# Projection chunks of 512 columns, kept split weights, and transposed x scaled on GpSimd in a one-core mixer step

## The chip, the cores and the metric

The kernel runs on one core of a Trainium2 chip. The metric is device time in microseconds for one execution; smaller is better. Five engines work side by side: PE (TensorE, matrix products), DVE (VectorE), ACT (ScalarE), POOL (GpSimd) and SP (SyncE, which here only issues transfers). Each engine runs its own list of instructions strictly in order, and waits for the others through semaphores.

## The reference, cut to what matters

```python
xn = rmsnorm(x, g_pre)                  # x: 2048 prompt tokens and 8x4 sample tokens, 1024 wide
proj = xn @ w_in                        # 1024 -> 38*128 columns
a_c, b_c, g_c, x_r, g_r, q, g_q = split(proj)       # 6, 6, 6, 6, 6, 4, 4 tiles of 128 columns
u = a_c * sigmoid(b_c)                  # then 31-tap depthwise conv, layernorm, silu, times silu(g_c)
...                                     # x_r: 4-tap conv, gates, linear recurrence, times silu(g_r)
...                                     # q: attention to 256 memory tokens, times silu(g_q)
out = concat([c, rr, o]) @ w_out        # 2048 -> 1024
y = x + rmsnorm(out, g_post)
```

All of it is float32, and besides y the new caches (the last conv rows, the recurrence state, memory keys and values) are outputs.

## The kernel before, in words

A float32 product is made of three products in a rounded type: each operand is split into a high part and a low rest, and `mm3` (L103) issues hi·hi, hi·lo and lo·hi into the same bank. `split` (L108) makes the parts: ACT copies the high part, DVE subtracts it from the source for the low part.

Phase 1 makes the projections and the three branches, in two parts of 1024 tokens; the first part also carries the 32 sample tokens. In each part the normalised x stands transposed (columns of x on the partitions) and split in `xh` and `xl`, in chunks of CW = 352 tokens (352, 352, 320; the last of the first part has 32 sample tokens more). `proj(m)` (L388) makes one 128-column tile of the projection: `load_w` (L236) loads 512 KB of raw weights on SP's queue, ACT and DVE split them into wh and wl, and for each chunk PE issues 8 k-steps of three matmuls into one PSUM bank; then an evacuation function runs. The tiles are named by their group: M_A, M_B (conv), M_GC, M_XR, M_GR, M_Q, M_GQ. There are 38 of them, so the weights are loaded and split 38 times in each part.

The x of the first part: the token rows of a chunk are loaded (`chunk_rows`), ACT sums their squares (`row_rs`, L213), DVE and POOL make the reciprocal root (L214, L215), DVE scales the rows (L221), PE transposes them eight times (L230), ACT and DVE take the split parts out of PSUM (L232, L233). The x of the second part: the row sums are made ahead (`part_stats`), x is loaded already transposed (`scaled_cols`, L346), DVE scales it with a broadcast row (L350), ACT and DVE split it (`split_cols`, L356, L357).

The order of the steps within a part is a string (ORDER): G is a conv tile pair with its GLU (`glu`), X, S, O belong to the recurrence, C is a conv gate (`conv_gate`), q and o are attention, M and V the memory keys and values, N the memory's normalisation, R the row sums of part 2; "G2:3" advances a step by three yields. G0 is the first step, and in it the tiles M_B and M_A run together, chunk by chunk. A scheduler that simulates the engines then sets each engine's own order; `high_priority` moves weight loads ahead. Pools of buffers (bufs=) decide when a tile's space comes free.

Branch results go to DRAM scratch (mixd, convd) through POOL's queue. Phase 2 (from 1035 us) keeps the split w_out resident and runs 17 blocks of tokens: output projection on 512 columns, norm, residual.

Of the kernel before, what the change touches and what calls it, by code (L numbers as in the profile page):

```python
# [32 lines left out]
EPS = 1e-6  # L33
CW = 352
CONV_LOW = 3000
MIX_HIGH = 500
# [3 lines left out]
NLC = 7  # L40
NCK = 5
NKC = 2
# [5 lines left out]
    "G0 N M1 X0:3 M0 X0:3 M2 X0:3 L X0 G1 G2:3 V G2 S0:2 S0:1 M3 S0:1 S0 C0 O0 C1 q0:3 G3:1 q0 G3 o0 R X1:7 X1 S1:1 G4 S1:1 S1:1 C2 C4 S1 O1 q1:3 G5:1 q1 G5:2 o1 G5 q3:3 C3:1 q3 C3 q2:3 o3:1 q2 o3 o2 C5",  # L48
    "G0:1 G0 s0 s1 p v0 X0 v1 G1 S0:1 G2:1 S0:1 G2 S0:1 S0 C0 O0 q0:3 G3:1 q0 G3:1 o0 G3 G4:3 X1 S1:1 G4 S1:1 S1 C1 O1 q1:3 G5:1 q1 G5 o1 q3:3 q2:1 q3 q2:2 o3:1 q2 o3 o2 C5 C4 C2 C3",
)  # L50
# [18 lines left out]
def hybrid_mixer_kernel(ctx, tc, x, xT, mem, consts, lnc, ccT, lcT, ckT, cv, w_in,  # L69
# [47 lines left out]
    def phase1():  # L117
# [117 lines left out]

        def load_w(src, ahead=None):  # L236
            with tc.high_priority(offset=W_HIGH if ahead is None else ahead):
                raw = pw.tile([P, KD, P], F32, tag="wr", name="wr", bufs=WR)
                sp.dma_start(raw, src)
                wh = pw.tile([P, KD, P], F32R, tag="wh", name="wh")  # L240
                wl = pw.tile([P, KD, P], F32R, tag="wl", name="wl")
                split(wh, wl, raw)
            return wh, wl
# [73 lines left out]
        def chunk_rows(part, c):  # L317
            alloc = flat_lc if c == len(part_chunks[part]) - 1 else big
            return load_rows([[x[t:t + w, :] for _, w, t in b] for b in row_blocks(part, c)], alloc)

# [15 lines left out]

        def scaled_cols(part, c):
# [3 lines left out]
            xs = [lc() for _ in range(3)]  # L341
            for a, w, tok in pieces(part, c, 0, n + ns):
                pool.dma_start(rb[:, a:a + w], rsd[0, tok:tok + w].partition_broadcast(P))
# [16 lines left out]
        for part in range(2):  # L360
            t0 = part * PART
            has_s = part == 0
            chunks = part_chunks[part]

            xh, xl = [], []
# [5 lines left out]
            ready[FIRST] = load_w(w_in[FIRST], 0)  # L371
            for c, (c0, n, ns) in enumerate(chunks):
                h = px.tile([P, KD, CW], F32R, tag="xh", name="xh")
                l = px.tile([P, KD, CW], F32R, tag="xl", name="xl")
                w = n + ns
                hi, lo = (lambda k: h[:, k, :w]), (lambda k: l[:, k, :w])
                if has_s:
                    if c + 1 < len(chunks):
                        rows[c + 1] = chunk_rows(0, c + 1)
                    if c == 0:  # L380
                        ready[M_A] = load_w(w_in[M_A], 0)
# [4 lines left out]
                xh.append(h)  # L386
                xl.append(l)
            def proj(m, evac):  # L388
                wh, wl = ready.pop(m) if m in ready else load_w(w_in[m])
                for c, (c0, n, ns) in enumerate(chunks):  # L390
                    w = n + ns
# [16 lines left out]
            def glu(i):  # L408
# [18 lines left out]
                def ev_a(c, ps):  # L427
                    ah = ck()
                    act.activation(ah[:, :ps.shape[1]], ps, AF.Copy, scale=0.5)
                    for dst, src in parts(c, ah):  # L430
                        dve.scalar_tensor_tensor(dst, dst, 1.0, src, op0=ALU.add, op1=ALU.mult)
# [53 lines left out]
            def lru_in(g):  # L485
                xrb = []
                lsb = LH + PART
                for i in range(3):
                    ch = 3 * g + i
                    xb = xslot()  # L490
                    sview = xb[:, lsb:].rearrange("p (b s) -> p b s", b=NB)
                    if has_s:
                        dve.memset(xb[:, :LH], 0.0)
                        sp.dma_start(sview[:, :, :LH], lcT[:, ch, :, :])
                    else:
                        act.activation(xb[:, :LH], xhist[:, ch, :], AF.Copy)

                    def ev(c, ps, xb=xb, sview=sview):
                        c0, n, ns = chunks[c]
                        act.activation(xb[:, LH + c0:LH + c0 + n], ps[:, :n], AF.Copy)  # L500
                        if ns:
                            act.activation(sview[:, :, LH:],
                                           ps[:, n:].rearrange("p (b s) -> p b s", b=NB), AF.Copy)

                    yield from proj(M_XR + ch, ev)
                    if has_s:
                        act.activation(xhist[:, ch, :], xb[:, PART:PART + LH], AF.Copy)
                        st_.dma_start(slconvT[:, ch, :, :], sview[:, :, NS:])
# [13 lines left out]
            def lru_scan(g):  # L522
# [13 lines left out]
                def prep(c):  # L536
                    c0, n, ns = chunks[c]
                    w = n + ns
# [30 lines left out]
                yield  # L569
                for c, (c0, n, ns) in enumerate(chunks):  # L570
                    w = n + ns
# [28 lines left out]
                    for i in range(3):  # L600
# [6 lines left out]
                        if ns:  # L607
# [5 lines left out]
                            dve.tensor_copy(xrb[i][1][:, :, :NS], hv)  # L613
                    if c + 1 < len(chunks):
                        nxt = prep(c + 1)
# [78 lines left out]
            def attn_o(h):  # L694
                kv, probs = att.pop(h)
                sg = {}

                def ev_g(c, ps):
                    c0, n, ns = chunks[c]
                    t = ck()  # L700
                    silu2(t[:, :n + ns], ps)
                    if ns:
                        act.activation(sgq[:, h, :], t[:, n:n + ns], AF.Copy)
                    sg[c] = t

                yield from proj(M_GQ + h, ev_g)
                ot = xslot()
                for q4 in range(2):
# [13 lines left out]
                    act.activation(ot[:, q4 * 512:(q4 + 1) * 512], po, AF.Copy)  # L722
                for c, (c0, n, ns) in enumerate(chunks):
                    dve.scalar_tensor_tensor(ot[:, c0:c0 + n], ot[:, c0:c0 + n], 0.5, sg[c][:, :n],
                                             op0=ALU.mult, op1=ALU.mult)
                st_.dma_start(mixd[:, 2 * NT + h, t0:t0 + PART], ot[:, :PART])
# [63 lines left out]
            def conv_gate(i):  # L790
                def ev(c, ps):
                    c0, n, ns = chunks[c]
                    t = pk.tile([P, CW], F32, tag="kc", name="kc", bufs=NKC)[:, :n + ns]
                    act.activation(t, ps, AF.Copy)
# [265 lines left out]
```

## Time and profile before

| | |
|---|---|
| times of three runs | 1429.36, 1429.61, 1431.13 us, median 1429.61 |
| the profiled execution's own time | 1426.34 us |
| its span in the trace | 1424.6 us |
| PE busy | 1405.8 us, 99% of the span |
| DVE, ACT, POOL busy | 1096.5, 681.3, 152.0 us |
| HBM traffic | 106 GB/s over the span |

The span is what the trace covers from first to last instruction; 1.7 us of the profiled execution's time lie around it, and that execution was 3.3 us shorter than the median of the three timed runs. Matmuls are pipelined: a matmul's row shows its whole latency, and the distance between the starts of two neighbours is what one more costs. The times below are microseconds from the span's start.

### The profile page before, as it was taken

To read this page: it belongs to the slowest core of one execution; us is meant where nothing else is said; L and a number is where in the kernel's file an instruction comes from. 1 tells how busy PE (TensorE), PEld (TensorE's weight loads), DVE (VectorE), ACT (ScalarE), POOL (GpSimd) and SP (SyncE) were. 2 spreads that over 40 slices of the span, in tenths; PEclk is the share of its full clock that TensorE was granted. 3 is DMA by queue.
4 is the path that set the end of the run, shared out by engine and by line. 5 is a ranking of instruction groups with operands and counts; after the bars stand their busy time and mean duration, and the time that the engine had idled before them with its cause. 6 is when DMAs were issued, how large, how long until landed. Compare 5 with 4: busy or idle time off the path is not lost.

```text
span 1424.6 us, 21056 instructions
## 1 busy us (share of the span) xinstructions
PE 1405.8 (99%) x8376; PEld 1316.8 (92%) x8376; DVE 1096.5 (77%) x1481; ACT 681.3 (48%) x1326; POOL 152.0 (11%) x233
## 2 busy tenths in 40 slices
PE   9999999999999999999999999999999999999997
PEld 8999999999999999899999999999987788888885
DVE  7797985989889998699989996999874664545532
ACT  7524688346754344238833369434453442332421
POOL 2101121011210101011100110000100000000000
PEclk9999999999999999999999999999999999999998
DMA  6243416132261214621122311421474432423310
GB/s 220 80 83 119 129 64 232 46 93 76 81 191 52 91 65 151 226 88 51 55 89 67 97 49 57 164 88 42 142 250 130 137 118 85 141 93 118 126 60 30
DMA packets 97282, 152.24 MB, mean 107 GB/s; under 512 B 15224, under 2 KB 66800, under 8 KB 97184
## 3 DMA queue, kind: packets, MB, share of 16 engines
q1 hardware_dynamic: 84528, 118.66, 26.5%
q0 software_dynamic: 12656, 32.25, 6.7%
q8 instruction: 65, 1.06, 0.3%
q14 instruction: 33, 0.27, 0.1%
HBM read 114.84 MB, written 36.04 MB: 106 GB/s over the span
## 4 chain that ended last, share of the span: by engine, by line
PE 87%; ACT 5%; DMA 3%; DVE 2%; issue 2%; SPq 0%; POOL 0%; DVEq 0%; POOLq 0%; ACTq 0%
PE bk L104 28%; PE bk L106 28%; PE bk L105 28%; ACT lc L579 1%; PE bk L914 1%; PE bk L714 1%; DMA lc<-in_xT 1%; DVE wl L110 1%; ACT wh L109 1%; DMA big<-in_x 1%; ACT lc L588 0%; ACT lc L584 0%; PE bk L750 0%; DMA lc<-in_x 0%; DMA wr<-in_w_mem 0%
## 5 line engine op out<-in xcount | busy, mean ns | idle before, releaser
L104 PE MATMUL bk<-xh,wh 128*128 128x352 f32 (+1 forms) x1824 | 584.6, 322 | 1.3 <-ACT xh L232 0.7
L105 PE MATMUL bk<-xl,wh 128*128 128x352 f32 (+1 forms) x1824 | 583.6, 320 | 0.0
L106 PE MATMUL bk<-xh,wl 128*128 128x352 f32 (+1 forms) x1824 | 583.0, 321 | 0.4 <-DVE wl L110 0.4
L465 DVE SCALAR_TENSOR_TENSOR big<-ub,cst,big 128x1024 f32<-128x1024 f32 x360 | 457.6, 1283 | 8.9 <-issue 4.4
L104 PEld LDWEIGHTS bk<-xh,wh 128*128 128x128 f32 x1824 | 342.1, 188 | 4.0 <-issue 1.4
L105 PEld LDWEIGHTS bk<-xl,wh 128*128 128x128 f32 x1824 | 343.7, 188 | 1.5 <-issue 0.6
L106 PEld LDWEIGHTS bk<-xh,wl 128*128 128x128 f32 x1824 | 342.6, 188 | 2.1 <-issue 0.8
L105 PE MATMUL bk<-wol,mh 128*128 128x512 f32 x512 | 201.6, 394 | 1.3 <-DVE wol L110 1.3
L104 PE MATMUL bk<-woh,mh 128*128 128x512 f32 x512 | 200.3, 392 | 0.0
L106 PE MATMUL bk<-woh,ml 128*128 128x512 f32 x512 | 199.4, 391 | 0.0
L109 ACT ACTIVATE wh<-wr 128x1024 fp32r<-128x1024 f32 x84 | 89.0, 1059 | 125.6 <-PE bk L105 111.1
L110 DVE TENSOR_TENSOR wl<-wr,wh 128x1024 fp32r<-128x1024 f32 x84 | 103.5, 1232 | 29.1 <-ACT wh L109 24.4
L105 PEld LDWEIGHTS bk<-wol,mh 128*128 128x128 f32 x512 | 96.3, 188 | 20.3 <-DVE wol L110 1.8
L106 PEld LDWEIGHTS bk<-woh,ml 128*128 128x128 f32 x512 | 96.2, 188 | 19.8 <-issue 0.8
L104 PEld LDWEIGHTS bk<-woh,mh 128*128 128x128 f32 x512 | 96.2, 188 | 19.5
L891 ACT ACTIVATE cr<-cr,lnv 128x128 f32<-128x128 f32 (+1 forms) x102 | 40.7, 478 | 150.8 <-DVE cr L889 150.8
L579 ACT ACTIVATE lc<-bk,hb 128x352 f32<-128x352 f32 (+3 forms) x144 | 77.0, 545 | 26.3 <-PE bk L106 23.7
L552 DVE SCALAR_TENSOR_TENSOR lc<-xr,cst,lc 128x352 f32<-128x352 f32 (+2 forms) x126 | 60.4, 522 | 4.6 <-ACT lc L548 4.6
L889 DVE TENSOR_TENSOR cr<-cr,bk 128x768 f32<-128x768 f32 (+1 forms) x17 | 15.6, 918 | 57.1 <-PE bk L888 57.1
L931 DVE TENSOR_TENSOR o<-bk,gpb 128x512 f32<-128x512 f32 (+1 forms) x34 | 23.3, 686 | 32.3 <-ACT sqj L930 32.2
L930 ACT ACTIVATE sqj<-bk 128x512 f32<-128x512 f32 (+1 forms) x34 | 20.1, 592 | 46.0 <-PE bk L106 45.2
L894 DVE TENSOR_TENSOR cr<-cr,mr 128x768 f32<-128x768 f32 (+1 forms) x17 | 15.7, 923 | 32.2 <-ACT cr L891 32.2
(242 smaller groups left out, 1696.2 us busy)
## 6 DMA issues: line engine op xcount, KB each, us to landing
wr<-in_w_in SPq DMA_DIRECT2D x76, 512.0 KB, 3.8
mr<-mixd SPq DMA_DIRECT2D x16, 1024.0 KB, 5.6
raw<-in_w_out SPq DMA_DIRECT2D x16, 512.0 KB, 4.6
xt<-in_x SPq DMA_DIRECT2D x16, 512.0 KB, 5.4
out_y<-xt SPq DMA_DIRECT2D x15, 512.0 KB, 2.7
convd<-big POOLq DMA_DIRECT2D x12, 512.0 KB, 2.9
mixd<-big POOLq DMA_DIRECT2D x12, 512.0 KB, 6.1
cr<-convd SPq DMA_DIRECT2D x16, 384.0 KB, 4.9
```

The source lines that it names most:

```text
L104: pe.matmul(ps, lh, rh, start=first, stop=False)
L105: pe.matmul(ps, lh, rl, start=False, stop=False)
L106: pe.matmul(ps, ll, rh, start=False, stop=last)
L109: act.activation(hi, src, AF.Copy)
L110: dve.tensor_tensor(lo, src, hi.bitcast(F32), op=ALU.subtract)
L465: dve.scalar_tensor_tensor(acc[:, :PART], ub[:, j:j + PART], cw[:, i, j:j + 1], acc[:, :PART], op0=ALU.mult, op1=ALU.add)
L552: dve.scalar_tensor_tensor(o, src(j), lw[:, ch, j:j + 1], o, op0=ALU.mult, op1=ALU.add)
L579: act.activation(dst[lo_:hi_, i, :], ps[lo_:hi_, :], AF.Tanh, scale=0.5, bias=hb[lo_:hi_, a, 3 * g + i:3 * g + i + 1])
L891: act.activation(cr[:, i, :], cr[:, i, :], AF.Silu, scale=lng[:, i:i + 1], bias=lnb[:, i:i + 1])
L894: dve.tensor_tensor(cr, cr, mr[:, :NT, :m], op=ALU.mult)
L930: act.activation(sqj[:m, :], ps[n][:m, :], AF.Square, scale=float(D ** -0.5), accum_out=ms[:m, n:n + 1])
L931: dve.tensor_tensor(o[:m, ns], ps[n][:m, :], gpb[:m, ns], op=ALU.mult)
```

## The change

Four things are changed together.

- The second part's projections run on two chunks of 512 tokens instead of three of 352, 352 and 320. `xh` and `xl` become one tile each, [128, 8, 1056], held in one buffer. The recurrence and the splitting of x stay on the 352 pieces (`subs`). The counts in ORDER's second string follow.
- In the first part, wh and wl are also stored to a DRAM scratch `wd`, 2 × 512 KB for each of the 38 tiles, on POOL's queue. The second part loads wh and wl from there on POOL's queue and splits nothing. The factor 0.5 of M_A is folded into the split weights, so its evacuation reads PSUM directly instead of a scaled copy that ACT made.
- In the first part, the x of the chunks 1 and 2 is loaded transposed. Their rows are still loaded and squared; `row_scales` spreads the scales over the partitions (DVE builds a diagonal, PE multiplies it by ones, ACT copies the bank to `rb`), POOL multiplies the transposed x by them, and ACT and DVE split the result. The 48 transposes and 6 row scalings of these chunks go.
- Smaller moves: the second part's stores go on SP's queue instead of POOL's, attention output is taken from PSUM by one DVE operation instead of ACT and DVE, the recurrence's cache rows pass through a small tile `lh`, and NCK is 4 instead of 5.

```diff
+    wd = dram.tile([M_GQ + HEADS, 2, P, KD * P], F32R, name="wd")
...
-    def split(hi, lo, src):
-        act.activation(hi, src, AF.Copy)
-        dve.tensor_tensor(lo, src, hi.bitcast(F32), op=ALU.subtract)
+    def split(hi, lo, src, scale=None):
+        if scale is None:
+            act.activation(hi, src, AF.Copy)
+            dve.tensor_tensor(lo, src, hi.bitcast(F32), op=ALU.subtract)
+        else:
+            act.activation(hi, src, AF.Copy, scale=scale)
+            dve.scalar_tensor_tensor(lo, src, scale, hi.bitcast(F32), op0=ALU.mult, op1=ALU.subtract)
...
+        def load_in(m, keep, ahead=None):
+            if keep:
+                wh, wl = load_w(w_in[m], ahead, 0.5 if M_A <= m < M_A + NT else None)
+                for i, t in enumerate((wh, wl)):
+                    pool.dma_start(wd[m, i], t.rearrange("p a b -> p (a b)"))
+            else:
+                wh = pw.tile([P, KD, P], F32R, tag="wh", name="wh")
+                wl = pw.tile([P, KD, P], F32R, tag="wl", name="wl")
+                for i, t in enumerate((wh, wl)):
+                    pool.dma_start(t.rearrange("p a b -> p (a b)"), wd[m, i])
             return wh, wl
...
+        proj_chunks = [part_chunks[0], [(c0, PC, 0) for c0 in range(0, PART, PC)]]
+        xh = px.tile([P, KD, PART + SAMP], F32R, tag="xh", name="xh")
+        xl = px.tile([P, KD, PART + SAMP], F32R, tag="xl", name="xl")
...
+        def row_scales(tiles, rb):
+            dg = ck()
+            ps = bank(ps_q, sum(n for _, n in tiles))
+            c0 = 0
+            for t, n in tiles:
+                rs = row_rs(t, n, xslot)
+                cs = slice(c0, c0 + n)
+                dve.tensor_scalar(dg[:n, cs], ident[:n, :n], rs[:n, :], None, op0=ALU.mult)
+                pe.matmul(ps[:, cs], ones[:n, :], dg[:n, cs], start=True, stop=True)
+                c0 += n
+            act.activation(rb[:, :c0], ps, AF.Copy)
...
-                dve.tensor_tensor(t[:, :k, :w], t[:, :k, :w], rb[:, :w].unsqueeze(1).broadcast_to([P, k, w]),
+                eng = pool if tiles else dve
+                eng.tensor_tensor(t[:, :k, :w], t[:, :k, :w], rb[:, :w].unsqueeze(1).broadcast_to([P, k, w]),
                                   op=ALU.mult)
...
-                    norm_rows(rows[c], xslot, KEEP if c == 0 else ())
-                    transposed(rows.pop(c), gp, hi, lo)
+                    if c == 0:
+                        norm_rows(rows[c], xslot, KEEP)
+                        transposed(rows.pop(c), gp, hi, lo)
+                    else:
+                        split_cols(scaled_cols(part, c, rows.pop(c)), gp, hi, lo)
...
-                wh, wl = ready.pop(m) if m in ready else load_w(w_in[m])
+                wh, wl = ready.pop(m) if m in ready else load_in(m, has_s)
                 for c, (c0, n, ns) in enumerate(chunks):
-                    w = n + ns
-                    ps = bank(ps_p, w)
+                    cs = slice(c0, c0 + n + ns)
+                    ps = bank(ps_p, n + ns)
                     for k in range(KD):
-                        mm3(ps, wh[:, k, :], wl[:, k, :], xh[c][:, k, :w], xl[c][:, k, :w],
+                        mm3(ps, wh[:, k, :], wl[:, k, :], xh[:, k, cs], xl[:, k, cs],
                             k == 0, k == KD - 1)
```

The order in which SP issues its transfers from the second weight tile on. `big` holds rows of x, `wr` raw weights, `lc` under the name in_xT the transposed x of the chunks 1 (three rows of 352 columns in all) and 2 (320 and 32).

Before:

```order
L239 DMA wr<-in_w_in 128x1024
L204 DMA lc<-in_x 128x1024 x2
L204 DMA lc<-in_x 64x1024
L204 DMA lc<-in_x 32x1024
L204 DMA lc<-in_mem 128x1024 x2
```

and now:

```order
L245 DMA wr<-in_w_in 128x1024
L384 DMA lc<-in_xT 128x3x352 x2
L384 DMA lc<-in_xT 128x2x352
L384 DMA lc<-in_xT 128x3x320 x2
L384 DMA lc<-in_xT 128x2x320
L384 DMA lc<-in_xT 128x3x32 x2
L384 DMA lc<-in_xT 128x2x32
L210 DMA lc<-in_mem 128x1024
L533 DMA lh<-in_lcT 128x24
L245 DMA wr<-in_w_mem 128x1024
L210 DMA big<-in_x 128x1024 x2
```

The rows of chunk 2, which came right behind the second weight tile, now stand behind the transposed x of both chunks, a memory block and a memory weight.

ACT at the start of the program, after its first squares (L219). L238 is the split of the transposed chunk 0, L465 the evacuation of M_B, L395 the split of the scaled chunks 1 and 2, L370 the copy to `rb`.

```order
L238 ACTIVATE xh<-bk,cst 128x352 x4
L370 ACTIVATE rb<-bk 128x352
L465 ACTIVATE ub<-bk 128x352
L395 ACTIVATE xh<-lc,cst 128x352 x8
L219 ACTIVATE xr,ms<-big 128x1024 x2
L465 ACTIVATE ub<-bk 128x352
L219 ACTIVATE xr,ms<-big 96x1024
L219 ACTIVATE xr,ms<-lc 128x1024
L370 ACTIVATE rb<-bk 128x352
L219 ACTIVATE xr,ms<-lc 128x1024
L534 ACTIVATE xr<-lh 128x8x3
L395 ACTIVATE xh<-lc,cst 128x352 x3
```

In the kernel before, all the squares of chunk 2 stand between the splits of chunk 1 and ahead of the first L425 (the evacuation of M_B's chunk 0); now the last of them stands behind the evacuation of chunk 1, and the copy to `rb` and the splits of chunk 2 behind that.

PE at the passage from chunk 1 to chunk 2 of the first two tiles, after the change. bk_451 is a bank of chunk 1, bk_477 and bk_504 are those of chunk 2, L368 the products that spread the row scales of chunk 2, L236 transposes of the memory tokens.

```order
L107 MATMUL bk_451<-xl_141,wh_165 128x352
L108 MATMUL bk_451<-xh_140,wl_166 128x352
L368 MATMUL bk_320<-ck_319,ones_70 128x128 x2
L368 MATMUL bk_320<-ck_319,ones_70 128x96
L236 MATMUL bk_560<-ident_65,lc_538 128x128
L236 MATMUL bk_565<-ident_65,lc_538 128x128
L236 MATMUL bk_570<-ident_65,lc_538 128x128
L236 MATMUL bk_575<-ident_65,lc_538 128x128
L106 MATMUL bk_477<-xh_140,wh_151 128x352
L106 MATMUL bk_504<-xh_140,wh_165 128x352
L107 MATMUL bk_477<-xl_141,wh_151 128x352
```

Before, eight groups of three transposes for each of chunks 1 and 2 stand between projection matmuls; now nothing but four transposes lies between the scales of chunk 2 and its first matmul.

## Rows read from the trace of the kernel before

**Rows 1.** The page's part 1, share of the span and instructions of each engine.

```profile
PE 1405.8 (99%) x8376; PEld 1316.8 (92%) x8376; DVE 1096.5 (77%) x1481; ACT 681.3 (48%) x1326; POOL 152.0 (11%) x233
```

**Rows 2.** PE's waits: engine, line, waited for, total us, times, longest.

```profile
PE bk L106 <- DVE xr L673: 2.0, 3, 1.0
```

**Rows 3.** PE's timeline in projections: start, us; first and last of 39, then 24.

```profile
799.77 0.32 PE L106 MATMUL bk<-xh,wl 128*128 128x352 f32 x1
...
805.89 0.32 PE L105 MATMUL bk<-xl,wh 128*128 128x352 f32 x1
1031.78 0.31 PE L104 MATMUL bk<-xh,wh 128*128 128x320 f32 x1
...
1035.12 0.31 PE L106 MATMUL bk<-xh,wl 128*128 128x320 f32 x1
```

**Rows 4.** PE's timeline in phase 2, first and last of 22 matmuls.

```profile
1251.23 0.39 PE L104 MATMUL bk<-woh,mh 128*128 128x512 f32 x1
...
1255.99 0.39 PE L104 MATMUL bk<-woh,mh 128*128 128x512 f32 x1
```

**Rows 5.** PE's timeline: G0's first and last matmul, transposes in it, and what follows.

```profile
13.57 0.43 PE L104 MATMUL bk<-xh,wh 128*128 128x352 f32 x1 [0.71 <-ACT xh L232]
...
23.90 0.47 PE L230 MATMUL bk<-ident,big 128*128 128x128 f32 x3
...
24.56 0.32 PE L105 MATMUL bk<-xl,wh 128*128 128x352 f32 x1
...
44.62 0.32 PE L106 MATMUL bk<-xh,wl 128*128 128x352 f32 x1
44.78 1.03 PE L230 MATMUL bk<-ident,lc 128*128 128x128 f32 x8
46.87 0.39 PE L104 MATMUL bk<-lc,wh 128*128 128x256 f32 x1 [1.05 <-ACT lc L232]
```

**Rows 6.** Busy us of each engine by stretch, granted clock, DMA share, GB/s.

```profile
0.00:4.00 4.00, 2.87 (x13) 2.87 (x14) 0.16 (x3) 1.28 (x1) 1.02 (x9) 1.00 0.56 193
4.00:20.00 16.00, 14.90 (x105) 14.06 (x104) 12.85 (x47) 13.84 (x26) 3.78 (x7) 1.00 1.02 353
560.00:1030.00 470.00, 469.31 (x3152) 460.29 (x3151) 416.93 (x509) 237.45 (x447) 49.55 (x70) 1.00 0.29 97
```

**Rows 7.** Groups of instructions by form: count, busy us, mean ns.

```profile
L592 DVE TENSOR_TENSOR lc<-lc 128x1056 f32<-128x1056 f32 x10 | 13.3, 1331 | 0.0
...
L561 POOL CAST ck<-lc 128x352 fp32r<-128x352 f32 x10 | 12.8, 1277 | 79.0 <-DVE lc L110 56.9 <-issue 10.4 <-DVE ub L431 8.7
...
L425 ACT ACTIVATE ub<-bk 128x352 f32<-128x352 f32 x24 | 11.2, 466 | 23.4 <-PE bk L106 23.3
...
L356 ACT ACTIVATE xh<-lc,cst 128x352 fp32r<-128x352 f32 x16 | 7.9, 579 | 0.0
...
L888 PE MATMUL bk<-dg,ones 128*128 128x128 f32 x32 | 6.2, 274 | 0.0
...
L215 POOL TENSOR_TENSOR rs<-rs,mhalf 128x1 f32<-128x1 f32 x8 | 5.4, 670 | 12.0 <-DVE rs L214 7.3 <-DVE spt L179 2.3 <-DVE xr L493 1.2
...
L886 DVE TENSOR_SCALAR dg<-ident,st 128x128 f32<-128x128 f32 x16 | 4.6, 286 | 9.9 <-POOL st L884 9.9
...
L213 ACT ACTIVATE xr<-big 128x1024 f32<-128x1024 f32 x4 | 4.2, 1058 | 3.1 <-DMA big<-in_x 3.1
```

**Rows 8.** Groups of instructions in 560 to 1030 us.

```profile
L110 DVE TENSOR_TENSOR wl<-wr,wh 128x1024 fp32r<-128x1024 f32 x36 | 44.7, 1242 | 10.2 <-ACT wh L109 10.2
```

**Rows 9.** Transfers: queue, count, KB each, median us from issue to landing.

```profile
mixd<-big POOLq DMA_DIRECT2D x12, 512.0 KB, 6.1
...
kv<-kvd POOLq DMA_DIRECT2D x8, 512.0 KB, 4.1
```

**Rows 10.** Busy us by stretch at the end, where PE has stopped.

```profile
1414.00:1416.00 2.00, 0.87 (x4) 0.38 (x2) 0.31 (x1) 0.69 (x2) 0.00 (x0) 1.00 0.00 0
1416.00:1418.00 2.00, 0.00 (x0) 0.00 (x0) 1.25 (x4) 0.00 (x0) 0.55 (x1) 0.71 0.00 0
```

More of the change, by code (lines that the diff above doesn't have):

```diff
@@ L34 @@
 CW = 352
+PC = 512
 CONV_LOW = 3000
@@ L40 @@
 NLC = 7
-NCK = 5
+NCK = 4
 NKC = 2
@@ L234, in transposed, with load_w @@
                                          op0=ALU.mult, op1=ALU.subtract)
-        def load_w(src, ahead=None):
+        def load_w(src, ahead=None, scale=None):
             with tc.high_priority(offset=W_HIGH if ahead is None else ahead):
@@ L241, in load_w @@
                 wl = pw.tile([P, KD, P], F32R, tag="wl", name="wl")
-                split(wh, wl, raw)
+                split(wh, wl, raw, scale)
+            return wh, wl
+        def load_in(m, keep, ahead=None):
[8 more added lines that the diff above has]
+                    pool.dma_start(t.rearrange("p a b -> p (a b)"), wd[m, i])
             return wh, wl
@@ L317, in chunk_rows @@
         def chunk_rows(part, c):
-            alloc = flat_lc if c == len(part_chunks[part]) - 1 else big
-            return load_rows([[x[t:t + w, :] for _, w, t in b] for b in row_blocks(part, c)], alloc)
+            return load_rows([[x[t:t + w, :] for _, w, t in b] for b in row_blocks(part, c)], big)
         def part_stats():
@@ L335, in part_stats, with scaled_cols @@
             pool.dma_start(rsd[0, PART:2 * PART].rearrange("(b p) -> b p", p=P), row)
-        def scaled_cols(part, c):
+        def row_scales(tiles, rb):
[9 more added lines that the diff above has]
+            act.activation(rb[:, :c0], ps, AF.Copy)
+        def scaled_cols(part, c, tiles=None):
             c0, n, ns = part_chunks[part][c]
@@ L341, in scaled_cols @@
             xs = [lc() for _ in range(3)]
+            if tiles:
+                row_scales(tiles, rb)
             for a, w, tok in pieces(part, c, 0, n + ns):
-                pool.dma_start(rb[:, a:a + w], rsd[0, tok:tok + w].partition_broadcast(P))
+                if not tiles:
+                    pool.dma_start(rb[:, a:a + w], rsd[0, tok:tok + w].partition_broadcast(P))
                 for i, t in enumerate(xs):
@@ L362, in phase1 @@
             has_s = part == 0
-            chunks = part_chunks[part]
-            xh, xl = [], []
+            st_ = pool if has_s else sp
+            subs = part_chunks[part]
+            chunks = proj_chunks[part]
             ready = {}
@@ L427, in ev_a @@
                 def ev_a(c, ps):
-                    ah = ck()
-                    act.activation(ah[:, :ps.shape[1]], ps, AF.Copy, scale=0.5)
-                    for dst, src in parts(c, ah):
+                    for dst, src in parts(c, ps):
                         dve.scalar_tensor_tensor(dst, dst, 1.0, src, op0=ALU.add, op1=ALU.mult)
@@ L493, in lru_in @@
                         dve.memset(xb[:, :LH], 0.0)
-                        sp.dma_start(sview[:, :, :LH], lcT[:, ch, :, :])
+                        hl = pt.tile([P, NB, LH], F32, tag="lh", name="lh", bufs=1)
+                        sp.dma_start(hl, lcT[:, ch, :, :])
+                        act.activation(sview[:, :, :LH], hl, AF.Copy)
                     else:
@@ L507, in lru_in @@
                         act.activation(xhist[:, ch, :], xb[:, PART:PART + LH], AF.Copy)
-                        st_.dma_start(slconvT[:, ch, :, :], sview[:, :, NS:])
+                        hl = pt.tile([P, NB, LH], F32, tag="lh", name="lh", bufs=1)
+                        act.activation(hl, sview[:, :, NS:], AF.Copy)
+                        st_.dma_start(slconvT[:, ch, :, :], hl)
                     else:
@@ L536, in prep @@
                 def prep(c):
-                    c0, n, ns = chunks[c]
+                    c0, n, ns = subs[c]
                     w = n + ns
@@ L569, in lru_scan @@
                 yield
-                for c, (c0, n, ns) in enumerate(chunks):
+                for c, (c0, n, ns) in enumerate(subs):
                     w = n + ns
@@ L613, in lru_scan @@
                             dve.tensor_copy(xrb[i][1][:, :, :NS], hv)
-                    if c + 1 < len(chunks):
+                    if c + 1 < len(subs):
                         nxt = prep(c + 1)
@@ L721, in attn_o @@
                             mh == 0, mh == 1)
[L722 to L725, printed above, removed]
+                    os_ = slice(q4 * 512, (q4 + 1) * 512)
+                    dve.scalar_tensor_tensor(ot[:, os_], po, 0.5, ot[:, os_], op0=ALU.mult, op1=ALU.mult)
                 st_.dma_start(mixd[:, 2 * NT + h, t0:t0 + PART], ot[:, :PART])
@@ L792, in ev @@
                     c0, n, ns = chunks[c]
-                    t = pk.tile([P, CW], F32, tag="kc", name="kc", bufs=NKC)[:, :n + ns]
+                    t = pk.tile([P, PC], F32, tag="kc", name="kc", bufs=NKC)[:, :n + ns]
                     act.activation(t, ps, AF.Copy)
```

29 lines of the change are left out of this document (11 added, 18 removed).

## The prediction

> **What bounds the kernel now.** I read the page's first part first: PE is busy for 1405.8 of 1424.6 us, and no other engine is above 77% [rows 1]. So I looked at PE's waits; the largest entry is 2.0 us in three waits [rows 2]. PE is the bound nearly from end to end. Removing work from DVE, ACT or POOL is therefore worth nothing by itself. Only two things can move the time: what PE's own instructions cost, and new waits of PE.
>
> So I read PE's timeline for the spacing of matmuls. In projections, 38 intervals of 352 columns take 6.12 us, 0.1611 each; 23 intervals of 320 columns take 3.34 us, 0.1452 each [rows 3]. In phase 2, 21 intervals of 512 columns take 4.76 us, 0.2267 each [rows 4]. [...]
>
> **Part by part: the wide chunks.** For one k-step and one of the three products, part 2 now takes 0.1611 + 0.1611 + 0.1452 = 0.4673 us, and with two of 512 columns 0.4533. The difference, 0.0140, times 38 tiles × 8 steps × 3 products = 912 gives **−12.8 us**. [...] I take 12.8, since the 512-column row is measured here, on the same three products of split operands.
>
> **The kept weights.** In the stretch 560 to 1030 DVE spends 44.7 us on the low parts of 36 weights [rows 8], and as many splits go from ACT. Both engines are hidden behind PE (469.31 of 470 busy, [rows 6]), so that is worth nothing. In their place each tile needs two 512 KB loads on POOL's queue. A tile's wh buffer is freed when PE leaves the tile before the last, so the load has the time of one tile, 48 × 0.2267 = 10.9 us. The nearest row, a 512 KB read from scratch on POOL's queue, takes 4.1 us from issue to landing [rows 9]; two in line, with the second behind the first, would take up to 8.2. That leaves at least 2.7 us: cost 0. If the cover is gone, each microsecond of lateness costs 36 to 38 us. In part 1 the stores (2 × 512 KB per tile; the same size takes 6.1 us to DRAM, [rows 9]) hold wh and wl no longer than the tile's own 11 us or so of matmuls; 97 GB/s are moved at a DMA share of 0.29 [rows 6], so there is room. Cost 0. POOL's list is in order, so where the weights for part 2's first two tiles stand behind the last store and behind convd's store, PE may wait once. I allow 0 to 1.5 us at the change of parts, as much again at phase 2, and take 0.
>
> **The start.** This is where I expect the loss. Removed from PE are the 16 groups of three transposes of chunks 1 and 2. One group with two matmuls takes 24.56 − 23.90 = 0.66 us [rows 5]; less 2 × 0.16 that is 0.34, and all are 5.4 us. These stand inside G0, which runs from 13.57 to 44.78.
>
> But chunk 2 becomes late. The order of SP's queue puts ahead of its rows: the rows of chunks 0 and 1 (1408 KB each), the constants (152), two weights (1024), the transposed x of both chunks (2816), memory rows and a memory weight (1024); with its own 1408 these are 9240 KB, or 9.46 MB. POOL's queue adds the stores of the first two split weights, 2.1 MB. The windows of the start give 193 GB/s for the first 4 us and 353 GB/s after, at a DMA share of 1.02, thus full [rows 6]: 0.77 MB by 4 us, the other 10.8 MB in 30.6 us. The rows land at about **34.7** (without the stores at 28.6).
>
> From there the chain is: ACT square 1.06, POOL root 0.67, DVE diagonal 0.29, PE product 0.27, ACT copy to `rb` (by the nearest ACT copy of 352 columns) 0.47, POOL scaling of the first 128x1056, ACT split 0.58 [rows 7]. The scaling has no row on POOL. From below it is DVE's 1.33 for the same shape and operation count; from above three times POOL's cast of 128x352, 3.83. I take 2.7: the cast is the nearer row in engine, but part of each cast must be a fixed start, which the larger one pays once. The sum is 6.0; seven hand-overs at an assumed 0.1 make it 6.7. Chunk 2 starts at 41.4.
>
> PE's work ahead of that ends earlier. Chunk 0 takes 48 × 0.161 = 7.7 us from 13.6 to 21.3; chunk 1 needs its transposed x (by the same sum, with one weight stored, at 20.5), a scaling and a split, so starts near 23.8 and ends near 32. PE then has only the scale products and four memory transposes until 41.4. Chunk 2's 48 matmuls last until 49.1. [...] I take 12 of them, at 0.16 more each, 2 us: 51.1 against 44.78. Some of the eight memory transposes (1.03 us, [rows 5]) are already done in the pause, −0.5. Sum: **+6 us**. Bounds: with a scaling of 1.33, no stores ahead and a full clock the chain starts at 33.9, and then the 5.4 us of removed transposes nearly pay for it, −3; with a scaling of 3.83 and twice the clock loss, +10.
>
> **Nothing on the path:** the folded 0.5, the direct evacuations, the tile `lh`, NCK 4 and the stores moved to SP are taken from engines that wait for PE. PSUM has four banks for projections, and a bank of 512 columns gives its evacuation 24 × 0.227 us instead of 24 × 0.161.
>
> **Sum.** −12.8 + 6 + 0 = −6.8, so the profiled execution would go from 1426.34 to 1419.5. It was 3.3 us below the median; against the median, 1429.61 − 6.8 = **1422.8 us**. 0.2% (2.9 us) is what a measurement of this kernel can tell from no change: faster is below 1426.7, slower above 1432.5. With the bounds of the boundaries the forecast's own range is 1420 to 1426.
>
> **Rivals.**
> 1. *The start hides it.* The rows of chunk 2 come before the stores, or the scaling is as quick as DVE's. Then the start costs −3 to +2, the time is 1414 to 1419, say **1417**. For it: the stores wait for the split and may lose the race for the DMA rings. Against: 9.46 MB alone need until 28.6. Chance 0.18.
> 2. *The start is worse.* POOL's scaling and DVE's low parts, both reading SBUF with two operands, take turns: eight low parts of chunk 1 at about 0.6 add up to 5 us to the three scalings, so the start costs +11: 1429.61 − 12.8 + 11 = **1428**. No row here shows DVE and POOL at it together. [...] Chance 0.14.
> 3. *The kept weights come late* (the other side). If the second half lands more than 10.9 us after its buffer is free, because of POOL's place in line or slower loads of the split type, every tile of part 2 waits. At 0.5 us each, 36 waits are 18 us: 1422.8 + 18 = **1441**. It decides from a lateness of 0.3 us (10 us in all) on. Against: 8.2 us from two rows of 4.1 in line. Chance 0.12.
> 4. *No surcharge to save.* If the spacing went with the columns, two of 512 would cost 2 × 0.2343 = 0.4685, nothing would be gained and the start would be lost: **1436**. Against it stand the three measured spacings. [...] Chance 0.03.
> 5. *POOL's order blocks a boundary*: a wait of 6 us for the first kept weights behind convd's store: **1429**. Chance 0.05.
>
> **The numbers.** The forecast has 0.48, rival 1 0.18: faster 0.66, with a little of rival 2 0.67. Rivals 2 and 5 are mostly within 0.2%: 0.18. Rivals 3 and 4: slower 0.15. The range 1416 to 1432 leaves out the lower end of rival 1 and rivals 3 and 4, together some 0.2.
>
> **What would show it.** Right: spacings of 0.227 us in part 2; PE idle between about 32 and 41 us before chunk 2, released by ACT's split behind POOL's scaling, with the granted clock below 1.00 after it; no wait of PE on wh or wl in part 2; the last projection matmul some 7 us earlier than 1035.12 [rows 3]. Wrong: PE waits on DMA wh or wl in many tiles of part 2 (rival 3); a G0 that ends by 45 (rival 1); POOL scalings much longer than 4 us beside DVE's low parts (rival 2).

## The result and the profile after

The changed kernel took **1445.06 us** (median) against 1429.86 before: ratio 1.0108, interval 1.0091 to 1.0125. It is 1.1% slower; 1422.8 us had been forecast, with a range of 1416 to 1432. One of the six executions took 4950 us at the full granted clock; it is not in the ratio, and without it the median is 1444.69.

The first part of the changed kernel's profile, and then the waits of PE (engine, line, waited for, total us, times, longest):

```profile
PE 1409.1 (98%) x7428; PEld 1233.1 (86%) x7428; DVE 1060.2 (74%) x1409; ACT 620.9 (43%) x1218; POOL 210.6 (15%) x343
...
PE bk L106 <- ACT xr L714: 5.1, 3, 2.7
PE bk L107 <- DVE xl L396: 3.2, 3, 1.4
PE bk L368 <- DVE ck L367: 2.1, 2, 1.8
...
PE bk L787 <- DMA ks<-in_ckT: 1.9, 1, 1.9
```

DVE and ACT lost the work they should [rows 1], yet PE, with 948 matmuls fewer, is busy 3.3 us longer. So the loss is only partly in waits. PE's timeline at five places (start, us, then the idle time before it): chunk 2's first matmul, the first of the memory keys, the first and last of 55 neighbours in part 2, and the last projection. `x1` is the number of instructions in a row.

```profile
44.70 0.66 PE L106 MATMUL bk<-xh,wh 128*128 128x352 f32 x1 [1.72 <-ACT xh L395]
...
57.59 0.39 PE L106 MATMUL bk<-lc,wh 128*128 128x256 f32 x1 [0.91 <-ACT lc L238]
...
1032.50 0.39 PE L108 MATMUL bk<-xh,wl 128*128 128x512 f32 x1
...
1045.03 0.40 PE L108 MATMUL bk<-xh,wl 128*128 128x512 f32 x1
...
1052.22 0.39 PE L108 MATMUL bk<-xh,wl 128*128 128x512 f32 x1
```

Three readings. The memory keys begin at 57.59 instead of 46.87 [rows 5]: the start lost 10.7 us. From there to the last projection it is 994.6 us instead of 1035.12 − 46.87 = 988.3 [rows 3, 5]: 6.4 us more, where 12.8 less were forecast. And the 512-column spacing is (1045.03 − 1032.50)/54 = 0.2320 us, not the 0.2267 of phase 2 [rows 4]. Two of them cost 0.4640, against 0.4673 for the three old chunks: 912 × 0.0033 = 3 us, where 12.8 were forecast.

The start in the changed kernel, by stretches (busy us of PE, its weight loads, DVE, ACT, POOL; granted clock; DMA share; GB/s):

```profile
30.00:36.00 6.00, 5.96 (x38) 5.67 (x36) 2.52 (x7) 1.15 (x2) 0.56 (x1) 1.00 1.04 305
36.00:40.00 4.00, 0.95 (x4) 0.60 (x4) 1.28 (x6) 3.61 (x7) 1.10 (x2) 1.00 0.61 205
40.00:44.00 4.00, 1.82 (x6) 1.21 (x6) 1.21 (x7) 1.69 (x5) 2.97 (x3) 0.53 0.01 2
44.00:48.00 4.00, 2.11 (x6) 1.66 (x7) 3.31 (x2) 3.39 (x7) 4.00 (x3) 0.50 0.00 0
48.00:52.00 4.00, 4.00 (x19) 3.74 (x18) 4.00 (x8) 1.07 (x2) 1.14 (x2) 0.69 0.01 4
```

PE stands nearly still from 36 to 44 us. The transfer rings are full (1.04 of what the 16 DMA engines can be busy) nearly until the rows are there; the granted clock is 0.53 of the full one in 40 to 44 us and 0.50 in 44 to 48, and it is back at 1.00 only from 51 us on. Where it is 0.50, neighbouring 352-column matmuls start 0.295 us apart (47.30 to 48.48), against 0.159 at 1.00 (51.91 to 53.34). The same stretch on POOL and DVE, around the scaling of chunk 1:

```profile
22.02 6.81 POOL L389 TENSOR_TENSOR lc<-lc,rb 128x1056 f32<-128x1056 f32 x3 [2.47 <-ACT rb L370]
...
21.95 0.17 DVE L189 SCALAR_TENSOR_TENSOR spt<-spt 128x6 f32<-128x6 f32 x1
22.15 2.37 DVE L190 TENSOR_SCALAR spt<-spt 128x6 f32<-128x6 f32 x1
24.43 0.16 DVE L191 TENSOR_SCALAR spt<-spt 128x6 f32<-128x6 f32 x1
```

POOL's first scaling starts at 22.02. DVE's next instruction, on six elements per partition, takes 2.37 us where its neighbours take 0.17: it ends at 24.52. By columns, the first scaling ends at about 22.02 + 6.81 × 1056/2816 = 24.57 (an estimate, since the three stand in one row). Two engines took turns here.

### The profile page after: what moved, and what is told of

Read it like the earlier page. It is cut to its first block, busy times and chain, and to the rows that moved or that the text cites. A ratio compares the mean times of both kernels' runs of the same rounds, so it can differ in the third digit from the quotient of the medians.

```text
span 1441.7 us, 19182 instructions
## 1 busy us (share of the span) xinstructions
PE 1409.1 (98%) x7428; PEld 1233.1 (86%) x7428; DVE 1060.2 (74%) x1409; ACT 620.9 (43%) x1218; POOL 210.6 (15%) x343
## 4 chain that ended last, share of the span: by engine, by line
PE 87%; DMA 4%; DVE 3%; ACT 2%; issue 2%; POOL 1%; SPq 0%; DVEq 0%; POOLq 0%; ACTq 0%
PE bk L106 28%; PE bk L108 28%; PE bk L107 28%; PE bk L951 1%; PE bk L753 1%; DMA lc<-in_x 1%; DMA ks<-in_ckT 1%; DVE big L503 1%; POOL lc L389 1%; DMA big<-in_x 1%; DMA wr<-in_w_mem 1%; DVE wl L113 0%; PE bk L787 0%; ACT lc L621 0%; DMA cst<-in_consts 0%
## 5 line engine op out<-in xcount | busy, mean ns | idle before, releaser
L106 PE MATMUL bk<-xh,wh 128*128 128x352 f32 (+1 forms) x1520 | 535.0, 353 | 3.5 <-ACT xh L395 2.1
L107 PE MATMUL bk<-xl,wh 128*128 128x352 f32 (+1 forms) x1520 | 535.0, 352 | 3.2 <-DVE xl L396 3.2
L108 PE MATMUL bk<-xh,wl 128*128 128x352 f32 (+1 forms) x1520 | 533.2, 352 | 0.3 <-DVE wl L116 0.3
L106 PEld LDWEIGHTS bk<-xh,wh 128*128 128x128 f32 x1520 | 286.5, 189 | 31.9 <-ACT xh L395 2.8
L107 PEld LDWEIGHTS bk<-xl,wh 128*128 128x128 f32 x1520 | 286.5, 189 | 30.4 <-DVE xl L396 4.5
L108 PEld LDWEIGHTS bk<-xh,wl 128*128 128x128 f32 x1520 | 286.4, 189 | 26.7 <-issue 1.2
L621 ACT ACTIVATE lc<-bk,hb 128x352 f32<-128x352 f32 (+2 forms) x144 | 77.4, 545 | 39.5 <-PE bk L108 37.2
L112 ACT ACTIVATE wh<-wr 128x1024 fp32r<-128x1024 f32 x40 | 42.3, 1059 | 99.7 <-PE bk L107 81.7
L113 DVE TENSOR_TENSOR wl<-wr,wh 128x1024 fp32r<-128x1024 f32 x40 | 49.4, 1236 | 12.8 <-ACT wh L112 12.7
L257 POOL DMA_DIRECT2D wd<-wh x38 | 20.7, 546 | 223.1 <-ACT wh L112 162.9
```

What stands on the lines that cost most here:

```text
L106: pe.matmul(ps, lh, rh, start=first, stop=False)
L107: pe.matmul(ps, lh, rl, start=False, stop=False)
L108: pe.matmul(ps, ll, rh, start=False, stop=last)
L257: pool.dma_start(wd[m, i], t.rearrange("p a b -> p (a b)"))
L621: act.activation(dst[lo_:hi_, i, :], ps[lo_:hi_, :], AF.Tanh, scale=0.5, bias=hb[lo_:hi_, a, 3 * g + i:3 * g + i + 1])
```

## The experiments

All times are medians; the ratios compare each with runs of the kernel before on the same chip (1428.7 to 1429.4 us). Two times of different batches can be off by some tenths of a microsecond for that reason.

**1. Do the matmuls depend on where their operands lie? (e1, e2, e3)** The first thought was the start of a tile: in the changed kernel wh, wl, xh and xl begin 64 bytes past a multiple of 128, in phase 2 woh and mh at one.

```diff
+        c1.tile([P, 16], F32, name="pad")     # e1, in the changed kernel; e2: 8 in the kernel before
         cst = c1.tile([P, CST_W], F32, name="cst")
...
         p2 = wp[-1]
+        p3.tile([P, 8], F32, name="pad", bufs=1)     # e3, in the kernel before
```

> The changed kernel with 64 unused bytes per partition ahead of the weight and x tiles, so that wh, wl, xh and xl start at multiples of 128 bytes (before: 64 past one). Nothing else differs. Theory A (a matmul's spacing depends on where its operands start in SBUF): the 512-column spacing of part 2 falls from 0.2320 to about 0.2270 us, 1824 matmuls are 9 us shorter, and the 352-column ones of part 1 may gain too: 1436 us or less against 1445. Theory B (projections of 512 columns are slower than phase 2's for another reason: bank use, evacuations, other engines): spacing stays 0.232, time 1445.

> The kernel before with 32 unused bytes per partition, so that its wh, wl, xh, xl start at multiples of 128 bytes (before: 96 past one). Theory A: the spacing of 352 and 320 columns falls too; if by the same 5 ns, 5472 matmuls are 27 us shorter (1402 us), if only long rows lose, near 1430. Theory B: 1430, spacing 0.160 and 0.146 as before.

> The kernel before with 32 unused bytes ahead of phase 2's tiles, so that woh, wol, mh and ml start 32 past a multiple of 128 bytes instead of at one. Theory A: the 512-column spacing of phase 2 rises from 0.2270 to about 0.232 us, 1536 matmuls, +8 us: 1438 us. Theory B: 0.2270 and 1430 us as before.

Measured: e1 1445.56 us (ratio 1.0112), spacing 0.2319; e2 1428.45 (0.9995, 0.9985 to 1.0004); e3 1430.11 (1.0007, 0.9998 to 1.0017), spacing 0.2275. Theory A fell: moving all tiles together changes next to nothing.

**2. The start undone (e4).** The first part's x of chunks 1 and 2 is normalised and transposed as before; the rest is as changed.

```diff
-            return load_rows([[x[t:t + w, :] for _, w, t in b] for b in row_blocks(part, c)], big)
+            alloc = flat_lc if c == len(part_chunks[part]) - 1 else big
+            return load_rows([[x[t:t + w, :] for _, w, t in b] for b in row_blocks(part, c)], alloc)
...
-                    if c == 0:
-                        norm_rows(rows[c], xslot, KEEP)
-                        transposed(rows.pop(c), gp, hi, lo)
-                    else:
-                        split_cols(scaled_cols(part, c, rows.pop(c)), gp, hi, lo)
+                    norm_rows(rows[c], xslot, KEEP if c == 0 else ())
+                    transposed(rows.pop(c), gp, hi, lo)
```

> The changed kernel with the old way for the x of chunks 1 and 2 in the first part: rows scaled on DVE, transposed on PE. Theory: the start (first matmul of the memory keys at 57.59 against 46.87 us) accounts for 10.7 us of the loss, so 1434 us, with the memory keys beginning near 47 us. Rival: the stores of the split weights take the transfer rings at the start anyway, so the rows stay late and only part (5 us) returns: 1440 us.

Measured: 1439.84 us (1.0073), memory keys at 52.53. The rival was right: half comes back, and another part of the change holds the start up.

**3. The distance between moving and stationary rows (e5, e8).** e1 to e3 had left one thing unchanged, the distance between the two operands of a matmul, the moving one (x in phase 1, w_out in phase 2) and the stationary one (the weights, and in phase 2 mh and ml). In the changed kernel xh lies 16384 bytes after wh, its rows 4224 bytes apart and those of wh 512; so the distance modulo 512 is 0, 128, 256 or 384, by k. In phase 2 woh and mh differ by multiples of 512 for all k. e5 gives part 2 a view with rows 4096 bytes apart:

```diff
+            xp, xq = (xh, xl) if has_s else (
+                t.rearrange("p a b -> p (a b)")[:, :KD * PART].rearrange("p (a b) -> p a b", a=KD) for t in (xh, xl))
...
-                        mm3(ps, wh[:, k, :], wl[:, k, :], xh[:, k, cs], xl[:, k, cs],
+                        mm3(ps, wh[:, k, :], wl[:, k, :], xp[:, k, cs], xq[:, k, cs],
```

> The changed kernel; in part 2 the rows of xh and xl lie 1024 columns apart instead of 1056 (the same tile, another view). All else as changed. Runs e1 to e3 moved x and weights together, so that the distance between the two did not change. Theory C: what counts is where the moving rows start relative to the stationary ones; in phase 2 the two differ by a multiple of 512 bytes for every k, in the changed part 2 by 0, 128, 256 or 384 past one. With 1024 they agree for every k: spacing 0.2320 to 0.2267 us, 1824 matmuls, -9.6 us, 1435 us. Theory D (a column costs 0.448 ns in phase 1 whatever the layout, with hardly a fixed part per matmul): spacing stays 0.232, 1445 us.

e8 does the opposite in phase 2 of the kernel before: 32 bytes in one pool, after woh6 to wol7 and before all the others.

```diff
+            if i % 2 == 0:
+                p3.tile([P, 8], F32, tag="pad", name="pad")
             mh = p3.tile([P, KM, P], F32R, tag="mh", name="mh")
```

> The kernel before with 32 unused bytes in one of phase 2's pools, so that the stationary mh and ml lie 32 bytes further relative to the moving woh6, wol6, woh7, wol7, and as before relative to all other woh and wol. Theory C: matmuls with woh6 to wol7 take some ns more than 0.2267 us, the others none. Theory D: none changes.

Measured, e5: **1433.10 us** (1.0027, 1.0011 to 1.0043), 12 us less than the changed kernel for a view (11, when each is held against its own runs of the kernel before). PE's timeline in e5, first and last of 231 neighbours:

```profile
777.47 0.40 PE L106 MATMUL bk<-xh,wh 128*128 128x512 f32 x1
...
829.65 0.40 PE L108 MATMUL bk<-xh,wl 128*128 128x512 f32 x1
```

52.18/230 = 0.2269. By these rows the spacing is worth 1824 × (0.2320 − 0.2269) = 9.3 us; PE is busy for 1398.4 us, 10.7 less. And e8 (1430.32 us, one run), in the middle of phase 2, where a block begins with woh6 and woh7:

```profile
1194.21 0.40 PE L105 MATMUL bk<-wol,mh 128*128 128x512 f32 x1
...
1196.77 0.40 PE L104 MATMUL bk<-woh,mh 128*128 128x512 f32 x1
...
1197.23 0.39 PE L106 MATMUL bk<-woh,ml 128*128 128x512 f32 x1
...
1201.99 0.39 PE L106 MATMUL bk<-woh,ml 128*128 128x512 f32 x1
```

The first 11 intervals take 2.56 us, 0.2327 each; the 21 from 1197.23 on 4.76 us, 0.2267 each. Over all blocks the matmuls with woh6 to wol7 are 0.2326 us apart, against 0.2268 in the kernel before, and the others 0.2275 against 0.2272. Theory C holds: it is the distance. (e8 is a single execution; the comparison is within its trace.)

**4. The parts alone (e6, e7, e9 to e12).** e7 is the wide chunks alone, with e5's view and the start of e4; the next ones add one part each to it. The folded 0.5, the direct evacuations, the tile `lh` and NCK 4 stay in it.

```diff
-            if keep:
-                wh, wl = load_w(w_in[m], ahead, 0.5 if M_A <= m < M_A + NT else None)
-                for i, t in enumerate((wh, wl)):
-                    pool.dma_start(wd[m, i], t.rearrange("p a b -> p (a b)"))
-            else:
...
-                    pool.dma_start(t.rearrange("p a b -> p (a b)"), wd[m, i])
+            wh, wl = load_w(w_in[m], ahead, 0.5 if M_A <= m < M_A + NT else None)
...
-            st_ = pool if has_s else sp
+            st_ = pool
```

> Only the wide chunks of the change: raw weights loaded and split in both parts as before, x of the first part made as before, all stores on POOL's queue as before; with the 1024-column view of e5. (The folded 0.5, the direct evacuations, the tile lh and NCK 4 stay.) Theory C: part 2's spacing 0.2267 and a saving of 12 us, with a start as before: 1417 us. Theory D: 1427 us. If the smaller edits that stay cost something, it shows as waits of PE in this run.

Measured: **1416.63 us**, ratio 0.9916 (0.9898 to 0.9934), the fastest version but for e13. The last projection starts at 1021.81 instead of 1035.12 [rows 3]; PE is busy for

```profile
PE 1395.1 (99%) x7464; PEld 1233.2 (87%) x7464; DVE 1093.8 (77%) x1447; ACT 656.8 (46%) x1254; POOL 143.1 (10%) x227
```

10.7 us less than before [rows 1]. Against its own runs of the kernel before it is 12.2 us faster, with the memory keys at 47.88, 1.0 later. So the wide chunks were worth about what was forecast, in another layout.

> Run e4 (old way for the x of chunks 1 and 2), and besides, the first two weight tiles are not stored to DRAM but loaded raw and split again in part 2. Theory: what e4 still lost at the start (memory keys at 52.5 against 46.9 us) comes from POOL's row scales standing behind the issue of these stores, which wait for the splits, and from 2.1 MB on full rings: memory keys near 47 us, 1434 to 1435 us against 1440. Rival: the late start in e4 has to do with x in one buffer or the rows' buffers: no change, 1440.

```diff
-            if keep:
+            if m in (FIRST, M_A):
+                wh, wl = load_w(w_in[m], ahead, 0.5 if m == M_A else None)
+            elif keep:
```

Measured, e6: 1440.05 us (1.0078). The memory keys begin at 48.50, 4.0 earlier than in e4, so the first two stores did hold up the start. The time did not move: PE's wait on the sample keys (ks) grew from 1.9 us in e4 to 4.3, and in the two traces the last projection is still 2.0 us earlier (1047.75 against 1049.78), of which the medians show nothing.

> Run e7 (wide chunks with the 1024-column view, 1416.6 us) plus the kept weights as in the change (stores in part 1, loads on POOL's queue and the other stores on SP's queue in part 2); the first part's x as before. It is run e4 with the 1024-column view. Theory: the kept weights cost about 11 us whatever else is changed (start +5, the waits of part 1 +3 to +6, the wait on the samples' keys in part 2 +2): 1427 to 1429 us. Rival: the kept weights cost only as part of the crowded start of the full change: 1418 to 1420 us.

e9, the undone start of e4 with e5's view: 1427.56 us (0.9985, 0.9973 to 0.9997). **Kept weights: +10.9 us.**

> Run e7 plus only the stores of wh and wl in part 1 (part 2 loads and splits raw weights as in e7, and leaves what was stored unread). Theory: the stores carry the loss of the start and of part 1, the loads and the moved stores that of part 2: part 1 ends as late as in e9, 1424 to 1426 us. Rival: the loads in part 2 are what costs: 1418 us.

e10 stores in part 1 and does not read: 1431.06 us (1.0009, 0.9996 to 1.0022), +14.4, more than either expectation. So the stores are what costs: e9, which also reads them back and moves part 2's other stores to SP's queue, is 3.5 us faster, not slower. One place is the start; the memory keys in e9 and e10 (47.88 in e7):

```profile
51.95 0.38 PE L106 MATMUL bk<-lc,wh 128*128 128x256 f32 x1 [0.88 <-ACT lc L238]
...
53.33 0.38 PE L106 MATMUL bk<-lc,wh 128*128 128x256 f32 x1 [0.88 <-ACT lc L238]
```

Another is the row sums of part 2, which part 1 makes. By stretch, the same 20 us of e7 and then of e10, and then one stretch of 5 us of each:

```profile
235.00:255.00 20.00, 18.85 (x122) 18.40 (x121) 14.82 (x31) 12.74 (x34) 3.98 (x6) 1.00 0.44 158
...
235.00:255.00 20.00, 16.31 (x97) 15.56 (x96) 13.36 (x37) 12.15 (x28) 8.08 (x13) 0.91 0.99 359
...
235.00:240.00 5.00, 4.63 (x32) 4.18 (x30) 2.59 (x10) 4.55 (x9) 3.86 (x6) 1.00 1.02 408
...
245.00:250.00 5.00, 2.25 (x15) 1.84 (x15) 2.10 (x3) 3.35 (x6) 1.62 (x3) 1.00 1.05 411
```

The DMA share goes from 0.44 to 0.99, but not because the rings were empty before: in e7 they are full too while the rows come (1.02 in 235 to 240), and then free (0.00 in 245 to 250). With the stores the full stretch lasts longer. ACT in e10 there (L345 squares the rows of part 2's x, L709 copies the attention queries), and PE:

```profile
242.08 1.06 ACT L345 ACTIVATE lc<-lc 128x1024 f32<-128x1024 f32 x1 [3.65 <-DMA lc<-in_x]
...
243.39 1.06 ACT L345 ACTIVATE lc<-lc 128x1024 f32<-128x1024 f32 x1 [0.15 <-DMA lc<-in_x]
...
246.11 1.06 ACT L345 ACTIVATE lc<-lc 128x1024 f32<-128x1024 f32 x1 [0.87 <-DMA lc<-in_x]
...
248.99 1.06 ACT L345 ACTIVATE lc<-lc 128x1024 f32<-128x1024 f32 x1 [0.78 <-DMA lc<-in_x]
...
250.05 0.44 ACT L709 ACTIVATE xr<-bk 128x352 fp32r<-128x352 f32 x1
...
250.54 0.58 PE L106 MATMUL bk<-kv,xr 128*128 128x256 f32 x1 [3.23 <-ACT xr L709]
```

The rows come late over full rings. ACT stands four times in front of squares that are in no hurry, 5.45 us in all. The query copy behind the last of them is in a hurry: PE waits 3.23 us for it, and the granted clock of the 20 us is 0.91.

> Run e7 plus only the transposed x scaled on POOL for the first part's chunks 1 and 2. Theory: the late rows, the row scales behind them and the scaling on POOL leave PE idle with a lower clock: the memory keys begin near 55 us against 47.9 in e7, 1423 to 1425 us. Rival: without the stores of the weights the rows come some 6 us earlier and the start costs nothing: 1417 us.

> Run e11 with the scaling on DVE in place of POOL. Theory 1 (the late rows carry the loss): as e11, less 2 x 1 us at most. Theory 2 (POOL's scaling and DVE's low parts hinder each other; in the changed kernel a low part took 0.83 to 1.0 us beside POOL's scaling against 0.63): memory keys 3 to 5 us earlier than in e11, low parts at 0.63 us, 1419 to 1421 us.

```diff
-                eng = pool if tiles else dve
+                eng = dve     # e12; e11 keeps the line above
```

e11: 1423.67 us (0.9961, 0.9942 to 0.9980), **new start: +7.0**, memory keys at 55.32. e12: 1419.63 (0.9931, 0.9915 to 0.9947), memory keys at 52.64. So about 4 of the 7 us go when the scaling leaves POOL (roughly: the five executions of e11 lie between 1420.5 and 1427.3). POOL's scaling of chunk 1 in e11 with DVE's low parts beside it, and the scaling and the low parts of chunk 2 in e12, where both are DVE's:

```profile
21.96 6.81 POOL L380 TENSOR_TENSOR lc<-lc,rb 128x1056 f32<-128x1056 f32 x3 [4.73 <-ACT rb L361]
...
25.50 1.72 DVE L387 SCALAR_TENSOR_TENSOR xl<-lc,cst,xh 128x352 fp32r<-128x352 f32 x1
...
27.15 2.02 DVE L387 SCALAR_TENSOR_TENSOR xl<-lc,cst,xh 128x352 fp32r<-128x352 f32 x1
...
29.08 1.07 DVE L387 SCALAR_TENSOR_TENSOR xl<-lc,cst,xh 128x352 fp32r<-128x352 f32 x2
...
37.71 3.23 DVE L380 TENSOR_TENSOR lc<-lc,rb 128x1056 f32<-128x1056 f32 x3 [0.22 <-ACT rb L361]
...
41.51 4.05 DVE L387 SCALAR_TENSOR_TENSOR xl<-lc,cst,xh 128x352 fp32r<-128x352 f32 x8
```

The two low parts that begin while POOL scales (21.96 to 28.77) take 1.72 and 2.02 us, the next two 1.07 together, and the eight in e12 0.51 each. But e12 takes away two things at once: the turns, and a scaling that is 3.6 us longer on POOL (6.81 against 3.23). How the 4 us divide between them was not separated.

**5. What was still open (e13, e14, e15).** e13 and e14 begin e7's view 64 and 16 columns later; e15 is e10 with wh alone stored, so it stores half of the data.

```diff
-                t.rearrange("p a b -> p (a b)")[:, :KD * PART]...
+                t.rearrange("p a b -> p (a b)")[:, 64:64 + KD * PART]...     # e13; e14: 16
...
-                for i, t in enumerate((wh, wl)):
+                for i, t in enumerate((wh,)):     # e15
                     pool.dma_start(wd[m, i], t.rearrange("p a b -> p (a b)"))
```

> Run e7 with part 2's view of xh and xl begun 256 bytes later, so that the moving rows start at 256 past a multiple of 512 bytes relative to the stationary ones, for every k. Open after e5 and e8: which distances are free. If only multiples of 512 are: spacing 0.232 us, 8 us more than e7 (1416.6), 1425. If multiples of 256 suffice: 0.2277 and 1417.

> As e13, but begun 64 bytes later. If only multiples of 256 or 512 bytes are free: spacing near 0.232 us and 1425. If the layout of e5 gained through the row distance of 4096 bytes and not through the start: 0.2277 and 1417.

> Run e10 (e7 plus stores, 1431.1 us) with only wh stored and not wl: half of the 38 x 1 MB. If the stores cost by filling the transfer rings where x rows are fetched at the same time (0.93 to 1.06 of the rings in 235 to 255 us, against 0.78 and 0.10 in e7), the loss against e7 falls by half or more: 1420 to 1424. If it is the store's place in POOL's line or the longer hold on the weight buffers, most of the loss stays: 1427 to 1430.

Measured: e13 1416.10 us (0.9909, 0.9893 to 0.9924), mean spacing in part 2 0.2277 as in e7: 256 bytes are free as well. e14 1419.72 (0.9938, 0.9918 to 0.9958), 0.2303: 64 bytes are not, though they cost only some half of what was expected; so the start counts and not the row distance. e15 1427.11 (0.9984, 0.9972 to 0.9996): with half of the data 10.5 of the 14.4 us stay. What comes back is at the start: the memory keys begin at 49.72, against 53.33 in e10 and 47.88 in e7. At the row sums nothing comes back: the rings are full all the same (1.01 and 1.02 in 235 to 240 and 240 to 245), and ACT stands 5.4 us for rows there, against 5.45 in e10. So the loss there doesn't follow the amount; whether full rings, the place in POOL's line or the longer hold on the weight buffers makes the rows late stays open.

## Why the prediction was wrong, step by step

- **Wide chunks, −12.8: the step that failed.** It took the 512-column spacing from phase 2, as "measured here, on the same three products of split operands". The layout differed: 0.2320 us came instead of 0.2267, some 3 us of gain instead of 12.8. e5 gives back 11 to 12 of the 22 us between forecast and result; e7 shows the term about right once the distance is. Rival 4 (chance 0.03) had the spacing nearly right, 2 × 0.2343 against 2 × 0.2320, by luck: it supposed that the spacing goes with the columns, and in e7 two of 512 take 2 × 0.2277 = 0.4554 us, against 0.4673 for the three old chunks. A warning stood in part 2 itself: 352 and 320 columns take 0.1602 and 0.1459 us there as means over all neighbours (intervals more than 10% off the median left out), and a line through them gives 0.2317 for 512. The few intervals of [rows 3] give 0.2406, too much. I compared with phase 2 instead.
- **Kept weights, 0: failed too.** The loads were hidden as forecast: PE waits for no wh or wl in part 2, rival 3 did not come. But I looked only at the buffers of the stores and at a mean DMA share of 0.29. The kept weights cost 11 us (e9), by their stores (e10), and before part 2: in e9 the memory keys begin 4.1 us later than in e7, and part 2's first 512-column matmul 11.4 us later (552.08 against 540.68). The traces show two stretches where the rings were already full without the stores: the start (1.02 of their time, [rows 6]), and the row sums of part 2 (1.02 in e7). What makes the rows late there beyond the amount stays open (e15).
- **The start, +6: the mechanism right, the size off.** 10.7 us in the full change, of which 7.0 remain with this part alone (e11); some of the rest is the stores' (4.1 in e9). The terms: last rows at 37.9 by ACT's third square, against 34.7; chunk 2 from 44.70, against 41.4, so the chain between took 6.8, against 6.7; in it the scaling near 2.5, against 2.7, an estimate: that part of POOL's cast is a fixed start was not shown. Nor does a run show the 0.1 us assumed for each hand-over; in the changed kernel those to DVE's diagonal, to PE's product and to POOL's scaling take 0.03, 0.05 and 0.07 (39.91 to 39.94, 40.21 to 40.26, 41.51 to 41.58). And chunk 2 took 11.4 us (to 56.07) instead of 9.7. In the 9.7, and doubled in the upper bound of +10, are 2 us for a lower clock, 12 matmuls at 0.16 more each, a term that no run shows: in the changed kernel the granted clock is 0.50 from 42 to 50 us, and where PE does not wait, chunk 2's matmuls lie 0.295 − 0.159 = 0.136 us further apart (13 are recorded up to 50.12).
- **Rival 2** (POOL and DVE take turns, 0.14) was true as a mechanism: the low parts, which have two operands in SBUF, took 1.72 and 2.02 us beside POOL's scaling in e11, against 0.51 in e12. Its price lies within the 4 us of e11 to e12, which also hold the slower scaling on POOL (6.81 against 3.23).
- **The sum.** From e7: 1416.6 + 7.0 (new start) + 10.9 (kept weights) + 12.0 (layout, e5 to the full change) = 1446.5, against 1445.1 measured. With each held against its own runs of the kernel before: −12.2 + 6.5 + 10.3 + 10.9 = +15.5, against +15.2.

## What to carry to other kernels

Take a matmul's spacing from a stretch with the same layout, and draw a line through two widths of one stretch, with means over many matmuls, before counting on a fixed cost per instruction: here the line gave 0.2317 for 512 columns, and 0.2320 came. When x and weights share SBUF, try row distances at which moving and stationary rows start a multiple of 256 bytes apart: 512-column matmuls took 0.2267 to 0.2277 us so, against 0.2320 in the changed kernel, and it was worth 11 to 12 us here, for a view. A mean DMA share hides the stretches in which more traffic lands on a full ring (in e7 0.44 over 235 to 255 us, with 1.02 in 235 to 240 and 0.00 in 245 to 250): look there for a load whose consumer stands in line, on its engine, ahead of something that PE needs.

## What was not expected of the hardware

- The spacing of 512-column matmuls followed the distance of their two operands in SBUF: 0.2267 to 0.2277 us at multiples of 256 bytes, 0.2303 at 64 past one (e14), 0.2326 at 32 (e8); 128 past one, alone, was not run with 512 columns. In the changed kernel every k was slow, 0.230 to 0.234, also those whose distance is free; why these don't run free between the others stays open. With 352 columns it is less: in the kernel before the distance is a multiple of 256 for even k and 128 past one for odd k, and the means (part 2 as it stands unchanged in e8) are 0.1594 and 0.1612.
- DVE's TENSOR_SCALAR on 128x6 with one SBUF operand took 2.37 us beside POOL's two-operand scaling; the same instruction takes 2.36 in e11, and 0.16 in e12 with POOL idle.
